# A two-layer encoder on one core: low parts of weights issued later, gate blocks reordered, convolution taps issued sooner

## The chip, the cores and the metric

One NeuronCore of a Trainium2 chip runs the whole program. The metric is the device time of one execution in microseconds (us). Engines are named as in the profile: PE (TensorE's matrix multiplies; PEld its weight loads), DVE (VectorE), ACT (ScalarE), POOL (GpSimd) and SP (SyncE, which issues the DMAs).

## What is computed

Two sequences, of 256 and 512 tokens and 1024 channels, go through the same two layers. A layer, cut to what matters here:

```
h = rms_norm(x);  q, k, v, u, gl = split(h @ w_in)
a = attention(rope(rms_norm(q)), rope(rms_norm(k)), v)         # 8 heads, 2 key heads
z = u[:1024] * sigmoid(u[1024:])                               # the gated input of the convolution
z = depthwise_conv(z, 31 taps) + b;  c = silu(layer_norm(z)) @ w_pw
x = x + (sigmoid(gl_a) * a + sigmoid(gl_c) * c) @ w_out
x = x + ffn(rms_norm(x))
```

All of it is fp32. A product is computed from split operands: each operand is a high part (rounded to the PE's fast format) and a low part (the rest), and three passes (high by high, low by high, high by low) go into one PSUM bank.

## The kernel before

Channels lie on the 128 partitions, in eight blocks of 128 channels; the 768 tokens lie along the free axis. The program is emitted by a planner (class Clock, line 54): it keeps a planned time `now`, moved on by each matmul's columns at 2400 per us, and a planned DVE time `dve`, moved on by each DVE operation (Vector, line 119: elements / 960 plus 0.13 us, of which a tap's addend is the constant TAP_MORE, line 1650). Every engine then runs its own instructions strictly in the order in which the planner put them out.

**Weights.** A weight block of 128 x 1024 is loaded into a stage tile by SP (Stage.load, line 227). Unit.make (line 240) then puts out, one right behind the other, a copy into the high part on ACT and a subtraction that makes the low part; for the blocks of the projections (names lo_L_wu, lo_L_wgl, lo_L_wqkv, lo_L_wpw) the subtraction is DVE's. `staged` counts the stages that are still in use, and load (line 313) issues the next one while there are fewer than four.

**The stream.** The projections are blocks in an order that FILL (line 1616) writes out by hand. "ag:j" makes channel block j of the convolution's gated input z: two weight blocks, each over all 768 tokens ("ag2" does j = 0 and 1). "gl:n" makes an output gate: one weight block; gates 0 to 7 belong to the heads, 8 to 15 to the convolution's output and go to DRAM. "k", "v" and "q:n" are the attention's projections. The first seven entries (BEFORE, line 1634) run before the attention. The others are its filling: the attention is 48 units (8 heads, 6 token tiles each, named h0t0 to h7t5), and behind the scores and again behind the transposes of each unit fill() (line 1386) puts out FILL_US / 2 planned us of the stream.

**A unit of the attention.** scores (line 1305): three matmuls on PE, the negated row maximum on DVE (L_hXtYst), Exp on ACT with a sum, the sum's reciprocal on POOL (line 1332), the scaling on ACT (L_hXtYp). flip (line 1336), one unit later: PE transposes the scaled block (L_hXtYT, line 207), ACT and DVE make its high and low parts. values (line 1355) multiplies by v and the gate.

**The convolution.** Each channel block needs 30 taps on DVE (conv, line 761: SCALAR_TENSOR_TENSOR on L_y, 128 x 783, in place), which go out in turn from at most two blocks' chains, as long as the planned DVE time is less than 1 us ahead of `now` (tick, line 76). There are three z tiles (N_Z, line 1668). An "ag" block first needs one of them:

Of the kernel before, what the change touches and what calls it, by code (L numbers as in the profile page):

```python
# [118 lines left out]
class Vector:  # L119
# [5 lines left out]
    def __getattr__(self, name):  # L125
        f = getattr(self.engine, name)

        def call(out, *args, **kw):
            n = 1
            for d in (args[0].shape if name == "tensor_reduce" else out.shape)[1:]:  # L130
                n *= d
            self.clock.vector(n / 960.0 + (TAP_MORE if n == CONV_N else 0.13))
            return f(out, *args, **kw)  # L133
# [22 lines left out]
def trunk(tc, x_in, x_tok, w_a, w_qkv, w_pw, w_out, w_gu, w_down, vecs, gqk, rope, y_out):  # L156
    nc = tc.nc
    clock = Clock()
    vector = Vector(nc.vector, clock)

    with ExitStack() as ctx:
# [48 lines left out]
        def act(out, in_, func=AF.Copy, **kw):  # L210
            nc.scalar.activation(out, in_, func, **kw)  # L211

        def sub_lo(engine, lo, x, hi):
            engine.tensor_tensor(lo, x, hi.bitcast(F32), op=ALU.subtract)  # L214
# [6 lines left out]
        class Stage:  # L221


            def __init__(self, name, src):
                self.name, self.src, self.tile, self.last = name, src, None, None
# [5 lines left out]
        class Unit:  # L231
# [2 lines left out]

            def __init__(self, name, stages):
                self.name, self.stages, self.out, self.live = name, stages, None, False
                for stage in stages:
                    stage.last = self

            def make(self, engines):  # L240
                hi = wpool.tile([P, 1024], F32R, name="hi_" + self.name, tag="w", bufs=N_W)
                lo = wpool.tile([P, 1024], F32R, name="lo_" + self.name, tag="w", bufs=N_W)
                stage = self.stages[0].tile
                act(hi, stage)
                n = 1024 // len(engines)
                for i, e in enumerate(engines):
                    sl = slice(i * n, (i + 1) * n)
                    sub_lo(e, lo[:, sl], stage[:, sl], hi[:, sl])
                self.out = (hi, lo)

        class Quarter(Unit):

# [6 lines left out]
            def make(self, engines):  # L259
                src = self.quad.operand(self.m)  # L260
                both = wpool.tile([P, 1024], F32R, name="wq_" + self.name, tag="w", bufs=N_W)
                hi, lo = both[:, :512], both[:, 512:]
                act(hi, src)
                sub_lo(engines[0], lo, src, hi)
                self.out = (hi, lo)

        class Quad:

# [19 lines left out]
        class Weights:  # L288
# [36 lines left out]
            def split(self, engines=(nc.gpsimd,)):  # L325
                w = self.all[self.ready]
                while not self.here(w):
                    assert self.load()
                assert self.live + w.size + max(self.staged, N_WS) <= N_W
                self.live += w.size  # L330
                w.live = True
                w.make(engines)
                self.staged -= sum(stage.last is w for stage in w.stages)
                self.ready += 1
                self.next = max(self.next, clock.now + W_STEP[w.size - 1])

            def pump(self):
                while self.load():
                    pass
                if self.ready < len(self.all) and clock.now >= self.next:  # L340
                    w = self.all[self.ready]
                    if self.here(w) and self.live + w.size + max(self.staged, N_WS) <= N_W:
                        self.split(self.engines(w))
# [5 lines left out]
            def get(self, w):  # L349
                while w.out is None:  # L350
                    self.split(self.engines(self.all[self.ready]))
                return w.out

            def free(self, w):
# [60 lines left out]
        weights = Weights()  # L415
# [217 lines left out]
        def layer_blocks(l):  # L633
# [127 lines left out]
            def conv(j, z):  # L761
                wcol = lambda k: vcol(l, V_WDW, k * KC + j)

                def first():
                    y.y[j] = UC(nm(f"y{j}"))
                    act(y.y[j], z[:, :CONV_N], AF.Identity, scale=wcol(0), bias=vcol(l, V_BDW, j))
# [23 lines left out]
                def ready():  # L790
                    first()
                    clock.at(FIRST_AT[1], lambda: clock.waiting.append(taps))
                clock.at(FIRST_AT[0], ready)

# [45 lines left out]
            def gl_body(idx):  # L840
                def body(ws):
# [3 lines left out]
                    for s, (t0, n) in enumerate(SPLITS):  # L845
                        pg = yield from proj_a(ws[0], y.hT, s, nm(f"gl{idx}_{s}"))
                        act(sg[:, t0:t0 + n], pg[:, :n])
                        if s == 0 and FILL[-1] == f"gl:{idx}":
                            y.h_free = 1
# [9 lines left out]

            for b in FILL:  # L860
                kind, _, n = b.partition(":")
# [435 lines left out]
        def attention(y):  # L1297
# [7 lines left out]
            def scores(n):  # L1305
# [22 lines left out]

                late = stream.done((l, FILL[-1]))
                jobs[n] = [  # L1330
# [55 lines left out]
            def fill():  # L1386
                goal[0] += FILL_US / 2
                if not stream.done((l, FILL[-1])):
                    stream.run(goal[0], (l, FILL[-1]))
                    if stream.done((l, FILL[-1])):  # L1390
                        goal[0] = stream.work
                        goal[0] += PW_START
                        y.late = clock.now + 8.0
                        y.h_free = 2
                        split_z(y)
                elif y.m_done:
                    goal[0] = max(goal[0] + (LATE_US - FILL_US) / 2, stream.work)
                    stream.run(goal[0], (l, f"pw:{min(y.m_done, PW_MAX) - 1}"))
# [21 lines left out]
        def channel_norm(y):  # L1420
# [59 lines left out]
            def scale(j):  # L1480
                def f():
                    for s, (t0, n) in enumerate(SPLITS):
                        sl = slice(YO[s], YO[s] + n)
                        vector.tensor_tensor(ys[j][:, sl], ys[j][:, sl], rstd[s][:, :n], op=ALU.mult)
                    if j in SILU_AT:
                        clock.at(0.5, lambda: silus(j))
                return f

            def silus(j1):
                split_z(y)  # L1490
                for j in range(y.silus, j1 + 1):
                    act(ys[j], ys[j], AF.Silu, scale=vcol(l, V_LNG, j), bias=vcol(l, V_LNB, j))
                    y.silus += 1
                    split_z(y)
                if y.silus == KC:
                    y.normed()
# [116 lines left out]
        clock.drain()  # L1613


FILL = ["ag2", "k", "q:0", "gl:0", "ag:4", "ag:2", "ag:3", "gl:8", "v", "gl:9", "gl:1", "q:1", "ag:5", "ag:6",
        "gl:10", "gl:2", "q:2", "ag:7", "gl:3", "gl:14", "gl:12", "gl:4", "gl:11", "q:3", "gl:5", "gl:13", "gl:7",
        "gl:15", "gl:6"]
SILU_AT = (5, 7)
FIRST_AT = (1.2, 1.4)  # L1620
BURSTS = ((1, 7), (6, 4), (5, 2), (3,))
D_FIRST = (4.0, 6.0)
# [11 lines left out]
BEFORE = 7  # L1634
SIG_MAX = 3
SIG_LEFT = 25
FILL_US = 6.3
LATE_US = 3.7
PW_MAX = 10
PW_START = 3.0  # L1640
# [6 lines left out]
RSTD_AFTER = 5.4  # L1647
TABLES_AT = 16.0
TAP_AHEAD = 1.0
TAP_MORE = 0.13  # L1650
W_STEP = (0.9, 2.9)
A_EXP = 2.2
A_REC = (3.5, 2.5)
# [91 lines left out]
```

If all three are in use (line 797), the taps of the oldest chains are put out at once, until one chain is finished; behind them POOL gets the three MEMSETs that clear the new tile's margins (line 803), which wait for the last tap of the chain that had the tile. When all eight chains have been added up (L_ysum), channel_norm (line 1420) puts out mean, squares, variance and scale with steps on PE, DVE, ACT and POOL. The first product with w_pw (pw_body, line 892) needs all of it: clock.force (line 99) puts out what is left.

## Time and profile before

| | us |
|---|---|
| median of 3 runs (2438.95 to 2444.44) | 2441.3 |
| the profiled execution | 2443.3 |
| its span on the core | 2441.5 |
| PE busy in the span | 2226.4 (91%) |
| DVE busy in the span | 1876.5 (77%) |

A row of a timeline gives the start and the length in us, the engine, the line, the operation, what it writes and reads, how many are merged into the row (x16), and in brackets how long the engine had been idle before it and what ended that. A row of the waits gives the engine that waited, for what, the us in total, how often, and the longest. "L_" stands for either layer.

### The profile page before, as it was taken

What the parts mean: (1) busy time and instruction counts of PE and PEld (TensorE: products, weight loads), DVE (VectorE), ACT (ScalarE), POOL (GpSimd) and SP (SyncE); (2) the same over time, 40 slices, a digit from 0 to 9 for tenths busy, and PEclk for the clock granted to TensorE, in tenths of its full rate; (3) what the DMA queues carried; (4) which work ended last, traced back from release to release, by engine and by line L of the source; (5) the groups of instructions that cost most, each with busy time, mean ns of one, the idle gap of its engine ahead of it and who ended that gap; (6) DMA issues with size and microseconds to landing.
All of it is one profiled execution on the core that took longest, in us unless ns stands there. A gap on an engine that the chain in (4) does not pass through costs nothing. (4 is left out here: it accounts for less than half of the span.)

```text
span 2441.5 us, 34896 instructions
## 1 busy us (share of the span) xinstructions
PE 2226.4 (91%) x13276; PEld 2095.6 (86%) x13276; DVE 1876.5 (77%) x2484; ACT 1143.8 (47%) x2289; POOL 1068.2 (44%) x935
## 2 busy tenths in 40 slices
PE   8999869949979999999989998698699799999997
PEld 7989859848979999999988898596589799999997
DVE  5899768956387788798968897689553877987888
ACT  5446536555244444444443555465642444444443
POOL 3704132311256666666445142131112666666663
PEclk9999989969989999999999999899799899999998
DMA  4112111213312343343421111112142133333332
GB/s 165 61 57 69 66 39 63 77 43 113 133 49 90 121 144 116 124 145 113 152 85 61 63 63 57 50 63 72 54 146 101 35 121 127 124 130 137 122 123 87
DMA packets 72423, 229.59 MB, mean 94 GB/s; under 512 B 8128, under 2 KB 15296, under 8 KB 72256
## 3 DMA queue, kind: packets, MB, share of 16 engines
q1 hardware_dynamic: 72256, 227.37, 27.1%
q8 instruction: 104, 1.70, 0.3%
q14 instruction: 63, 0.52, 0.1%
HBM read 208.46 MB, written 18.87 MB: 93 GB/s over the span
## 5 line engine op out<-in xcount | busy, mean ns | idle before, releaser
L133 DVE SCALAR_TENSOR_TENSOR L_y<-L_z,vec,L_y 128x783 f32<-128x783 f32 x480 | 496.1, 1077 | 0.8
L214 POOL TENSOR_TENSOR wq_L_wgu_0m<-T_L_wgu,wq_L_wgu_0m 128x512 fp32r<-128x512 f32 x168 | 228.6, 1376 | 173.8 <-ACT wq_L_wgu_0m L211 173.8
L211 ACT ACTIVATE wq_L_wgu_0m<-T_L_wgu 128x512 fp32r<-128x512 f32 x168 | 102.7, 630 | 259.3 <-DVE T_L_wgu L133 208.7
L214 POOL TENSOR_TENSOR wq_L_wgu_0m<-st_L_wgu,wq_L_wgu_0m 128x512 fp32r<-128x512 f32 x126 | 179.3, 1425 | 43.4 <-ACT wq_L_wgu_0m L211 42.7
L203 PE MATMUL L_gl<-L_h1h,hi_L_wgl 128*128 128x512 f32 (+1 forms) x512 | 176.6, 345 | 0.0
L203 PE MATMUL L_gl<-L_h1h,lo_L_wgl 128*128 128x512 f32 (+1 forms) x512 | 173.2, 338 | 0.0
L203 PE MATMUL L_gl<-L_h1l,hi_L_wgl 128*128 128x512 f32 (+1 forms) x512 | 172.9, 338 | 0.0
L203 PEld LDWEIGHTS L_gl<-L_h1h,lo_L_wgl 128*128 128x128 f32 x512 | 97.0, 189 | 11.0
L203 PEld LDWEIGHTS L_gl<-L_h1l,hi_L_wgl 128*128 128x128 f32 x512 | 97.2, 190 | 9.2
L203 PEld LDWEIGHTS L_gl<-L_h1h,hi_L_wgl 128*128 128x128 f32 x512 | 97.0, 190 | 9.1
L203 PE MATMUL L_c<-L_zsl,hi_L_wpw 128*128 128x256 f32 (+1 forms) x256 | 89.2, 348 | 9.5 <-DVE L_zsl L133 9.5
L203 PE MATMUL L_c<-L_zsh,hi_L_wpw 128*128 128x256 f32 (+1 forms) x256 | 92.1, 360 | 4.6 <-ACT L_zsh L211 4.6
L203 PE MATMUL L_ug<-L_h1h,lo_L_wu 128*128 128x256 f32 (+1 forms) x256 | 89.0, 348 | 2.8 <-DVE lo_L_wu L133 2.8
L133 DVE TENSOR_TENSOR L_dl<-L_silu,L_dh 128x384 fp32r<-128x384 f32 x80 | 59.5, 783 | 41.0 <-ACT L_dh L211 41.0
L203 PE MATMUL L_ug<-L_h1h,hi_L_wu 128*128 128x256 f32 (+1 forms) x256 | 90.6, 354 | 0.0
L203 PE MATMUL L_ua<-L_h1h,lo_L_wu 128*128 128x256 f32 (+1 forms) x256 | 88.6, 346 | 1.4 <-DVE lo_L_wu L133 1.4
L203 PE MATMUL L_ua<-L_h1h,hi_L_wu 128*128 128x256 f32 (+1 forms) x256 | 89.7, 350 | 0.0
L203 PE MATMUL L_ug<-L_h1l,hi_L_wu 128*128 128x256 f32 (+1 forms) x256 | 89.5, 349 | 0.0
L211 ACT ACTIVATE wq_L_wgu_0m<-st_L_wgu 128x512 fp32r<-128x512 f32 x126 | 78.5, 623 | 22.8 <-POOL wq_L_wgu_0m L214 19.8
L203 PE MATMUL L_c<-L_zsh,lo_L_wpw 128*128 128x256 f32 (+1 forms) x256 | 88.9, 347 | 0.0
L203 PE MATMUL L_ua<-L_h1l,hi_L_wu 128*128 128x256 f32 (+1 forms) x256 | 88.1, 344 | 0.0
L203 PE MATMUL L_o<-L_mTlo,hi_L_wo 128*128 128x384 f32 x256 | 86.4, 338 | 0.0
(1630 smaller groups left out, 7626.7 us busy)
## 6 DMA issues: line engine op xcount, KB each, us to landing
st_L_wgu<-w_gu SPq DMA_DIRECT2D x88, 512.0 KB, 3.5
st_L_wu<-w_a SPq DMA_DIRECT2D x32, 512.0 KB, 3.5
st_L_wgl<-w_a SPq DMA_DIRECT2D x32, 512.0 KB, 3.5
st_L_wqkv<-w_qkv SPq DMA_DIRECT2D x24, 512.0 KB, 3.5
st_L_wpw<-w_pw SPq DMA_DIRECT2D x16, 512.0 KB, 3.5
st_L_wo<-w_out SPq DMA_DIRECT2D x16, 512.0 KB, 3.6
g_dram<-L_sgl SPq DMA_DIRECT2D x16, 384.0 KB, 3.0
L_gj<-g_dram SPq DMA_DIRECT2D x16, 384.0 KB, 3.8
```

The lines of the kernel that those rows point to most:

```text
L133: return f(out, *args, **kw)
L203: nc.tensor.matmul(out, lhsT, rhs, start=start, stop=stop)
L211: nc.scalar.activation(out, in_, func, **kw)
L214: engine.tensor_tensor(lo, x, hi.bitcast(F32), op=ALU.subtract)
```

## The change

Four things. The low part of a weight unit whose subtraction is DVE's no longer goes out right behind the high part, but LO_AFTER = 1.6 planned us later, or at the latest when the unit is first asked for (get); the stage counts as in use until then. In FILL "gl:8" goes in front of "ag:3" (so it takes its place among the seven blocks before the attention, and "ag:3" becomes the first filling), "ag:6" goes behind "gl:10", and "ag:7" goes behind "gl:3" and "gl:14". FILL_US goes from 6.3 to 6.5. TAP_MORE goes from 0.13 to 0.02, so the planner counts a tap as 0.836 us (783 / 960 + 0.02) where it counted 0.946.

```
+                self.low = lambda: None
...
-                for i, e in enumerate(engines):
-                    sl = slice(i * n, (i + 1) * n)
-                    sub_lo(e, lo[:, sl], stage[:, sl], hi[:, sl])
+
+                def low():
+                    for i, e in enumerate(engines):
+                        sl = slice(i * n, (i + 1) * n)
+                        sub_lo(e, lo[:, sl], stage[:, sl], hi[:, sl])
+                    weights.used(self)
+
                 self.out = (hi, lo)
+                if engines == (vector,):
+                    self.low = clock.later(LO_AFTER, low)
+                else:
+                    low()
...
-                self.staged -= sum(stage.last is w for stage in w.stages)
                 self.ready += 1
                 self.next = max(self.next, clock.now + W_STEP[w.size - 1])
+
+            def used(self, w):
+                self.staged -= sum(stage.last is w for stage in w.stages)
...
                 while w.out is None:
                     self.split(self.engines(self.all[self.ready]))
+                w.low()
                 return w.out
...
-FILL = ["ag2", "k", "q:0", "gl:0", "ag:4", "ag:2", "ag:3", "gl:8", "v", "gl:9", "gl:1", "q:1", "ag:5", "ag:6",
-        "gl:10", "gl:2", "q:2", "ag:7", "gl:3", "gl:14", "gl:12", "gl:4", "gl:11", "q:3", "gl:5", "gl:13", "gl:7",
+FILL = ["ag2", "k", "q:0", "gl:0", "ag:4", "ag:2", "gl:8", "ag:3", "v", "gl:9", "gl:1", "q:1", "ag:5",
+        "gl:10", "ag:6", "gl:2", "q:2", "gl:3", "gl:14", "ag:7", "gl:12", "gl:4", "gl:11", "q:3", "gl:5", "gl:13", "gl:7",
         "gl:15", "gl:6"]
+LO_AFTER = 1.6
...
-FILL_US = 6.3
+FILL_US = 6.5
...
-TAP_MORE = 0.13
+TAP_MORE = 0.02
```

## Rows read from the trace of the kernel before

**Rows 1.** The page, part 1: busy us, share of the span and instructions of each engine
```profile
PE 2226.4 (91%) x13276; PEld 2095.6 (86%) x13276; DVE 1876.5 (77%) x2484; ACT 1143.8 (47%) x2289; POOL 1068.2 (44%) x935
```
**Rows 2.** What PE waited for: us in total over both layers, times, longest
```profile
PE L_h3t0T L207 <- ACT L_h3t0p L211: 42.6, 2, 21.3
PE L_var L203 <- DVE L_sq L133: 40.3, 2, 20.1
...
PE L_h1t5T L207 <- ACT L_h1t5p L211: 13.0, 2, 6.5
...
PE L_h7t4T L207 <- ACT L_h7t4p L211: 2.3, 2, 1.1
```
**Rows 3.** Timeline of POOL, layer 0, around the wait of 21.3 us
```profile
339.29 0.20 POOL L803 MEMSET L_z<- 128x15 f32 x3 [19.29 <-DVE L_y L133]
...
344.59 0.54 POOL L1332 TENSOR_TENSOR L_h3t0st<-L_h3t0st,nones 128x1 f32<-128x1 f32 x1
```
**Rows 4.** Timeline of DVE, the same stretch
```profile
324.03 15.20 DVE L133 SCALAR_TENSOR_TENSOR L_y<-L_z,vec,L_y 128x783 f32<-128x783 f32 x16
...
346.65 1.23 DVE L133 TENSOR_TENSOR lo_L_wgl<-st_L_wgl,hi_L_wgl 128x1024 fp32r<-128x1024 f32 x1 [6.21 <-ACT hi_L_wgl L211]
```
**Rows 5.** Timeline of POOL, layer 0, ahead of the wait of 6.5 us
```profile
256.31 0.20 POOL L803 MEMSET L_z<- 128x15 f32 x3 [12.74 <-DVE L_y L133]
```
**Rows 6.** Busy us by stretch: PE, PEld, DVE, ACT, POOL, PEclk, DMA share, GB/s
```profile
100.00:240.00 140.00, 137.66 (x901) 124.59 (x899) 129.81 (x163) 64.28 (x143) 42.11 (x49) 1.00 0.20 66
240.00:380.00 140.00, 112.18 (x700) 100.47 (x699) 100.70 (x126) 70.69 (x146) 29.23 (x39) 0.90 0.15 51
380.00:484.00 104.00, 104.00 (x679) 94.22 (x678) 94.50 (x117) 59.67 (x130) 33.19 (x32) 1.00 0.22 74
```
**Rows 7.** Timeline of PE, layer 0, from the end of the stream to w_pw
```profile
484.43 1.56 PE L203 MATMUL L_mean<-L_ysum,ones 128*128 128x256 f32 x4 [0.18 <-DVE L_ysum L133]
506.10 2.72 PE L203 MATMUL L_var<-ones,L_sq 128*128 128x2 f32 x12 [20.11 <-DVE L_sq L133]
...
520.56 0.58 PE L203 MATMUL L_c<-L_zsl,hi_L_wpw 128*128 128x256 f32 x1 [4.74 <-DVE L_zsl L133]
```
**Rows 8.** Timeline of PE behind the wait of 21.3 us
```profile
346.64 0.63 PE L203 MATMUL L_ug<-L_h1l,hi_L_wu 128*128 128x512 f32 x1
347.06 0.63 PE L203 MATMUL L_ug<-L_h1h,lo_L_wu 128*128 128x512 f32 x1
...
350.19 0.39 PE L203 MATMUL L_ug<-L_h1l,hi_L_wu 128*128 128x512 f32 x1
350.43 0.39 PE L203 MATMUL L_ug<-L_h1h,lo_L_wu 128*128 128x512 f32 x1
```
**Rows 9.** Timeline of PE, two 256-column matmuls of a gl block
```profile
272.31 0.28 PE L203 MATMUL L_gl<-L_h1h,hi_L_wgl 128*128 128x256 f32 x1
272.43 0.28 PE L203 MATMUL L_gl<-L_h1l,hi_L_wgl 128*128 128x256 f32 x1
```
**Rows 10.** Timeline of DVE: the row maxima of units h4t0 and h4t5
```profile
387.71 0.42 DVE L133 TENSOR_REDUCE L_h4t0st<-L_h4t0s 128x1 f32<-128x256 f32 x1 [0.40 <-PE L_h4t0s L203]
...
433.39 0.68 DVE L133 TENSOR_REDUCE L_h4t5st<-L_h4t5s 128x1 f32<-128x512 f32 x1
```
**Rows 11.** What DVE waited for: low parts behind their high parts
```profile
DVE lo_L_wgl L133 <- ACT hi_L_wgl L211: 44.6, 18, 6.2
...
DVE lo_L_wu L133 <- ACT hi_L_wu L211: 14.9, 12, 2.4
...
DVE lo_L_wqkv L133 <- ACT hi_L_wqkv L211: 11.9, 10, 2.1
```
**Rows 12.** Timeline of PE, layer 0: a low part that is used as it ends
```profile
101.71 0.39 PE L203 MATMUL L_ua<-L_h1h,lo_L_wu 128*128 128x256 f32 x1 [0.57 <-DVE lo_L_wu L133]
```
**Rows 13.** Timeline of POOL, layer 0, where the attention begins
```profile
151.41 0.20 POOL L803 MEMSET L_z<- 128x15 f32 x3 [17.77 <-DVE L_y L133]
162.03 0.55 POOL L1332 TENSOR_TENSOR L_h0t0st<-L_h0t0st,nones 128x1 f32<-128x1 f32 x1 [10.41 <-ACT L_h0t0p L211]
```

More of the change, by code (lines that the diff above doesn't have):

```diff
@@ L265, in make @@
                 self.out = (hi, lo)
+                weights.used(self)
         class Quad:
```

## The prediction

> **What bounds the kernel now.** I read the page's busy shares first: PE works for 2226 of 2441.5 us [rows 1], so only PE's idle time, some 215 us, can be won by moving work about. Then the list of what PE waited for. Its two longest entries lie in both layers, at the same places and of the same length: 21.3 us in front of the transposes of unit h3t0 and 20.1 us in front of the variance; a wait of 6.5 us at h1t5 is third in this phase [rows 2]. The timelines of POOL and DVE say what they are.
>
> The wait at h3t0 is the planner's own. Block "ag:7" needs a z tile while three are in use, so the planner puts out the taps of the oldest chains at once: 16 taps in one run of 15.2 us [rows 4]. POOL meets the MEMSET of the new tile first, waits 19.29 us for the last tap, then does a q block's rotary work, and only at 344.59 the reciprocal of h3t0 that was queued behind it [rows 3]. ACT's scaling and PE's transposes need that reciprocal. What follows is as dear: the planned DVE time is now far ahead, so no taps go out for a while, and DVE idles 6.21 us in front of a low part [rows 4]. The wait at h1t5 has the same cause, "ag:6": the MEMSET waits 12.74 us, DVE's queue is full of taps, the unit's maximum comes late, and with it the reciprocal [rows 5].
>
> The busy time by stretch shows what this does to DVE. In 100 to 240 it is idle for 10.2 of 140 us, in 380 to 484 for 9.5 of 104, but in the stretch with the two waits, 240 to 380, for 39.3 of 140 [rows 6]. That matters because the stream and the convolution end together: PE's last gate block is done at 484.4 and PE waits only 0.18 us for L_ysum. Behind it comes the channel norm's own chain, during which PE has nothing: 20.11 us for the variance and more up to 520.6 [rows 7]. So two chains reach 484 side by side, and both have to come sooner.
>
> **The change part by part.**
>
> *The z tiles asked for later.* How much later is worked out from the code's columns and the trace. Planned lengths at 2400 columns per us: a gl block 8.2, an ag block 16.4, a q or v block 15.4 us. On the chip 512 columns take about 0.24 and 256 about 0.12 us from start to start [rows 8, 9], so a gl block (24 of each) takes 8.6 and PE is some 10% slower than planned. A unit takes (433.39 - 387.71) / 5 = 9.1 us [rows 10], of which 6.3 x 1.1 = 6.9 are filling, so 2.2 are its own. Filling in front of "ag:7": before 5 gl, v and two q, 2 ag = 120 us, or 19.0 units of 6.3; after 6 gl, three qkv, 3 ag = 144 us, or 22.2 units of 6.5. Counted from the program's start, the block has two gl blocks more in front of it ("gl:8" and "ag:3" only change places) and 3.2 units more: 17.2 + 7.0 = 24 us later in PE's work. "ag:6": one gl and 2.2 units, 13.4 us later. "ag:5" comes one unit later, 2 us. The MEMSETs waited 19.29 and 12.74 us [rows 3, 5]. In the 24 us DVE has about 7 us of other work more (two low parts of 1.23 [rows 4], 3.2 units of some 1.4), which leaves 17 us for taps; it also wins back idle time in 240 to 324. So the forced runs are gone, or a few taps long. Bounds for the two waits together, per layer: all 27.8 us go (the half of 42.6 and 13.0 [rows 2]), or half of it stays, if the chains are late all the same. I take all, and put remains under new waits.
>
> *The clock.* Behind the wait of 21.3 us the 512-column matmuls start 0.42 apart until 349.6 and then 0.23 to 0.24 [rows 8]: the granted clock fell to its lower level (1.2 of 2.4 GHz; 0.90 in the mean of this stretch [rows 6]). Some eight matmuls lost 0.2 us each. With the same behind h1t5, about half as long, 3 us per layer go. Bounds 0 and 4.
>
> *DVE has to keep pace.* Its work from 100 to 484 is 129.8 + 100.7 + 94.5 = 325 us [rows 6], and the change adds and removes none. At the idle share of the two undisturbed stretches (19.7 of 244 us, 8%) it needs 353.5 us and ends at 453.5: 30.5 us sooner, just what PE gains (27.8 + 3). So the stretch of the norm behind it stays as it is. Two edits can make DVE faster still. **Low parts later:** DVE waits 44.6 + 14.9 + 11.9 us for high parts of gl, u and qkv blocks over both layers [rows 11], since a low part is queued right behind its high part. With taps in between, part of that goes. **Taps sooner:** one tap takes 15.20 / 16 = 0.95 us [rows 4]. The planner counted 0.946, which on a PE 10% slower than planned leaves DVE short of work; 0.836 fills that. Together at least nothing, at most about 14 us per layer (the undisturbed stretches' share of the waits on high parts). But DVE only has to win where PE then waits less in the norm; I take 4 per layer.
>
> *What gets later.* A low part 1.6 us later is followed by whatever DVE has queued, and PE waits for it only where it is used at once: 0.57 us at 101.71 [rows 12], one of two such places in a layer. At each it can cost 1.6 us and a tap of 0.95, or save the 0.57. The stage's release and so the next load on SP come 1.6 us later too, in front of stores that nothing awaits. "ag:3"'s MEMSET now lies on POOL in front of h0t0's reciprocal; its chain should end at about 151 as now, well before that is due (162) [rows 13]. Its sigmoid falls among the units' exponentials. A fuller DVE queue makes maxima later; the nearest rows are small waits such as h7t4's 1.1 us [rows 2]. Bounds per layer 0 and 10; I take 4. FILL_US keeps the filling at 37 units (242 / 6.5 against 234 / 6.3) although "ag:3" joined it, so the end of the attention keeps its form. The FFN only has its two plain down units touched; nothing.
>
> **Sum.** Per layer -27.8 - 3 - 4 + 4 = -31; twice, -62. Against the profiled execution's 2443.3 us that is 2381; that execution lies 2.0 above the median, so 2379 by the runs. I say 2380.
>
> **The rivals.**
>
> *The wait moves to the norm.* PE comes 31 us sooner, DVE does not, because taps are held back by something else (z gated late, sigmoids flushed late). For it: the two chains end together now [rows 7], so any wait that PE loses and DVE does not comes back there. Against it: 39 of 59 idle us lie in the disturbed stretch [rows 6]. If DVE ends only 12 us sooner, the layers win 12 each: 2417. Chance 0.17.
>
> *The change does not do what it says:* the z tiles come no sooner at the new place, as the chain in front started later too, and half of the 27.8 us reappears at another unit. Then 14 + 2 per layer: 2409. Chance 0.07.
>
> *Slower: the planned norm overtakes the chip.* The planner counts each tap 0.11 us too short; over 240 taps DVE can fall 26 us behind the plan. L_mean and L_var [rows 7] would then stand in PE's queue in front of the last gate blocks, and PE, in order, would wait out the lag and the 20 us there with that filling queued behind. Price: 20 us of filling per layer that now runs before the norm runs after it. It decides if DVE wins back less than 20 of its 59 idle us; with 10 won it is +10 per layer, 2461. Against it: PE is 10% slower than planned, which takes up most of the lag. Chance 0.07. [...]
>
> *Nothing measurable,* gains and new waits equal: 0.04.
>
> **How the numbers follow.** A measurement of this kernel can tell about 0.2%, 4.9 us. The forecast has 0.65, in its own range 2355 to 2403: the lower end if DVE's extra feed shortens the norm's wait by 12 per layer and nothing new appears, the upper if new waits cost 10 per layer and 6 more of the old ones stay. The range that holds 8 in 10 goes on to 2426, past the first two rivals' times, and starts at 2352. Faster: 0.65 + 0.17 + 0.07 = 0.89, of which I keep 0.01 for the slower side, as their prices are unsure; same 0.04; slower 0.07 + 0.01.
>
> **What would show it.** In the profile after, PE's waits at h3t0 and h1t5 are gone or below 3 us; POOL's MEMSET waits in the attention are short; DVE's idle time between the start of the attention and L_ysum falls from 59 to some 30 us; L_mean runs near 453; the wait at L_var is 14 to 20 us. The forecast is wrong if a wait of over 10 us stands in front of another unit, if L_var's wait grows to 35 us, or if L_mean waits for L_ysum with gate blocks left.

## The result, and the profile after

The changed kernel takes 2336.15 us in the median of four runs (2335.30 to 2336.96), where the kernel before took 2442.55 beside it (four runs, 2438.95 to 2444.44). The ratio is 0.9566 with a 95% interval of 0.9549 to 0.9583: faster by 106 us. The forecast had the sign but 62 us only, and the time lies below its range, 2355 to 2403. The profiled execution of after took 2336.18 us, with a span of 2334.4.

The first part of the page, the busy time by engine, answers to [rows 1]:

```profile
PE 2213.9 (95%) x13276; PEld 2087.3 (89%) x13276; DVE 1880.3 (81%) x2484; ACT 1160.7 (50%) x2303; POOL 1085.7 (47%) x935
```

PE does the same 13276 matmuls. Its busy time fell by 12.5 us, beside a granted clock whose mean over the span rose from 0.959 to 0.982 of full speed, and the span by 107.1, so its idle time fell by 94.6. Where, the list of PE's waits says, which answers to [rows 2] (us over both layers, times, longest):

```profile
...
PE L_c L203 <- ACT L_zsh L211: 9.7, 2, 4.8
PE L_c L203 <- DVE L_zsl L133: 9.5, 2, 4.7
...
PE L_h1t3T L207 <- ACT L_h1t3p L211: 6.1, 2, 3.5
...
PE L_h4t5T L207 <- ACT L_h4t5p L211: 4.8, 2, 2.9
...
PE L_h0t0T L207 <- ACT L_h0t0p L211: 3.0, 2, 1.6
```

The waits at h3t0 and h1t5 are gone, as forecast. But the third long one of before, 20.1 us per layer in front of the variance, is gone as well, and of that the forecast took away 4. PE's timeline in layer 0, against [rows 7], shows how:

```profile
432.12 1.45 PE L203 MATMUL L_mean<-L_ysum,ones 128*128 128x256 f32 x4
...
458.44 1.40 PE L203 MATMUL L_var<-ones,L_sq 128*128 128x2 f32 x12
...
466.44 0.82 PE L207 MATMUL L_rstd<-ident,L_rb 128*128 128x128 f32 x6
...
472.10 0.58 PE L203 MATMUL L_c<-L_zsh,hi_L_wpw 128*128 128x256 f32 x1 [4.85 <-ACT L_zsh L211]
```

L_mean stood at 484.43 and now stands at 432.12, 52 us sooner. No bracket stands behind L_mean, L_var and L_rstd: PE had other work in front of each, because the stream's last gate block ends only at 466.2. The norm's chain is no faster (26.3 us from L_mean to L_var, 21.7 before; 40.0 from L_mean to the first product with w_pw, 30.8 before), but it runs beside that work, where before it ran behind it with nothing else to do. DVE's last step of the convolution, in its timeline:

```profile
427.44 0.97 DVE L133 TENSOR_TENSOR L_ysum<-L_ysum,L_y 128x783 f32<-128x783 f32 x1
```

The busy time by stretch, against [rows 6] (columns as there):

```profile
100.00:240.00 140.00, 132.68 (x873) 120.39 (x872) 132.20 (x164) 64.04 (x141) 42.25 (x48) 1.00 0.19 62
240.00:380.00 140.00, 139.80 (x883) 125.54 (x882) 132.79 (x164) 89.95 (x176) 41.39 (x42) 0.99 0.20 67
380.00:426.00 46.00, 43.12 (x300) 39.97 (x299) 44.12 (x55) 29.01 (x71) 25.42 (x25) 0.96 0.20 72
```

DVE idles 7.8 + 7.2 + 1.9 = 16.9 us from 100 to 426; before it was 59 up to 484. The convolution's end came 56 us sooner: some 42 us by less idle time, and 14 because less of DVE's other work lies ahead of it by then, most of it the attention's (36 row maxima had run before, 31 now) and weights' low parts.

### The profile page after: what moved, and what is told of

Its sections match the earlier page's. It is cut to its first block, busy times and chain, and to the rows that moved or that the text cites. A ratio compares the mean times of both kernels' runs of the same rounds, so it can differ in the third digit from the quotient of the medians.

```text
span 2334.4 us, 34909 instructions
## 1 busy us (share of the span) xinstructions
PE 2213.9 (95%) x13276; PEld 2087.3 (89%) x13276; DVE 1880.3 (81%) x2484; ACT 1160.7 (50%) x2303; POOL 1085.7 (47%) x935
## 3 DMA queue, kind: packets, MB, share of 16 engines
q1 hardware_dynamic: 72256, 227.37, 28.6%
## 5 line engine op out<-in xcount | busy, mean ns | idle before, releaser
L133 DVE SCALAR_TENSOR_TENSOR L_y<-L_z,vec,L_y 128x783 f32<-128x783 f32 x480 | 502.0, 1084 | 1.7
L203 PE MATMUL L_o<-L_mThi,hi_L_wo 128*128 128x384 f32 x256 | 86.8, 339 | 0.3 <-ACT L_mThi L211 0.2
```

The lines of the kernel that those rows point to most:

```text
L203: nc.tensor.matmul(out, lhsT, rhs, start=start, stop=stop)
```

## The experiments

Two theories went into them. **"Two waits"** is the forecast's: the later z tiles remove the two waits, the taps and the low parts are worth some 4 us per layer. **"Early end"** was formed on the profile after: the convolution now ends well ahead of the stream, so the norm's chain hides, and it is the taps and the low parts that bring that end forward.

### The three parts, alone and in pairs

The order (here the new FILL together with FILL_US 6.5), the short taps (TAP_MORE 0.02) and the later low parts were put into the kernel before one at a time, and taken out of the changed one, one at a time. The edits, in this order:

```
e1_order_only  before, with the new FILL and      -FILL_US = 6.3    +FILL_US = 6.5
e2_taps_only   before, with                       -TAP_MORE = 0.13  +TAP_MORE = 0.02
e3_low_only    before, with the low-part edit:    +self.low = clock.later(LO_AFTER, low) ...
e4_no_taps     after, with                        -TAP_MORE = 0.02  +TAP_MORE = 0.13
e5_no_low      after, with           -if engines == (vector,):      +if False:
e6_no_order    after, with the old FILL and       -FILL_US = 6.5    +FILL_US = 6.3
```

> The kernel before with the new order of the filling and FILL_US 6.5, old taps, old low parts. Theory 'two waits' (the forecast's: the order takes 27.8 + 3 us per layer, taps and low parts are worth 4 or less): 2375 to 2385 us, the waits at h3t0 and h1t5 below 3 us, and a wait for the variance of 15 to 20 us per layer as before. Theory 'early end' (the convolution now ends some 40 us ahead of the stream, so that the channel norm runs under filling, and it is the taps and the low parts that bring the end forward): 2365 to 2385 us, and again 10 to 20 us of wait for the variance. If the order alone brings the end forward: 2335 to 2350 us and no wait for the variance.

> The kernel before with TAP_MORE 0.02 alone. Theory 'two waits': the waits at h3t0 and h1t5 stay within 3 us of their 21.3 and 6.5 us, at most 4 us per layer come from a shorter norm: 2434 to 2444 us. Theory 'early end': the plan puts more taps out ahead of 'ag:7', so fewer are forced there, and the convolution ends sooner: 2395 to 2425 us, the wait for the variance below 12 us per layer.

> The kernel before with the later low parts alone. Theory 'two waits': 2436 to 2444 us, the waits at h3t0, h1t5 and for the variance as before. Theory 'early end' as the runs now have it (the short planned taps decide when the convolution ends, low parts keep DVE from standing behind ACT and so shorten the units' chains; with the new order they gave 23 us without the short taps and 29 us with them): 2410 to 2430 us, L_mean 5 to 15 us sooner than 484, and still a wait of 15 to 21 us for the variance.

> The changed kernel with the old TAP_MORE 0.13. Theory 'two waits': at most 4 us per layer are lost, 2336 to 2344 us. Theory 'early end': the planner counts each of the 240 taps 0.11 us longer, 26 us per layer, so the convolution ends up to 26 us later, near the end of the stream, and part of the norm lies bare again: 2350 to 2376 us with 5 to 20 us of wait for the variance per layer.

> The changed kernel with every low part queued right behind its high part again. Theory 'two waits': DVE's waits for high parts come back (18 us more in front of the low parts of gl blocks alone, per layer), which costs at most 4 us per layer: 2336 to 2344 us. Theory 'early end': DVE loses some 20 us per layer of feed, but the convolution has about 40 us of room to the end of the stream, of which the norm's chain needs most: 2340 to 2360 us, with a wait for the variance of 0 to 10 us per layer.

> The changed kernel with the old order of the filling and FILL_US 6.3. Theory 'two waits': the waits at h3t0 and h1t5 come back nearly whole, 2390 to 2400 us or more. Theory 'early end': the short taps alone left 4.1 and 1.5 us at these two units, the low parts take off 23 to 29 us of the 2379 us of the short taps alone: 2348 to 2362 us, no wait for the variance, L_mean at 430 to 440, so the order is worth 12 to 26 us only and not the 54 that the forecast gave it.

Measured:

| in the kernel | us | ratio to before, interval |
|---|---|---|
| the order alone (e1) | 2403.3 | 0.9837 [0.9821, 0.9854] |
| short taps alone (e2) | 2379.4 | 0.9737 [0.9722, 0.9751] |
| later low parts alone (e3) | 2425.1 | 0.9926 [0.9912, 0.9941] |
| order and low parts (e4) | 2380.4 | 0.9745 [0.9730, 0.9759] |
| order and taps (e5) | 2364.7 | 0.9681 [0.9667, 0.9696] |
| taps and low parts (e6) | 2341.5 | 0.9589 [0.9575, 0.9603] |

The order, which the forecast made the heart of the change, is worth 39.8 us alone and only 5.3 on top of the other two, which is about what can be told apart. The short taps are worth 63.7 alone and 44.3 on top; the low parts 17.5 alone and 28.6 on top. "Two waits" missed all six times, by 10 us or more. "Early end" has e3 in its range and was near the others: e4 and e5 came out 4 and 5 us above theirs, e6 and e2 7 and 16 us below, so the taps are worth more than it had said. e1 was 18 us slower than either had it: its wait for the variance stayed as both said, but it has new waits that neither counted.

What each leaves of PE's waits says why. The order alone (e1):

```profile
PE L_var L203 <- DVE L_sq L133: 37.3, 2, 18.7
...
PE L_h1t3T L207 <- ACT L_h1t3p L211: 12.5, 2, 6.3
PE L_h6t4T L207 <- ACT L_h6t4p L211: 9.5, 2, 4.7
...
PE L_mean L203 <- DVE L_ysum L133: 6.7, 2, 3.3
```

The waits at h3t0 and h1t5 are gone, but the one for the variance is not, and three new ones take 14.3 us per layer. The new order didn't make the z tiles wholly free in time. POOL's MEMSETs for "ag:6" and "ag:7" in e1, against 12.74 us [rows 5] and 19.29 us [rows 3]:

```profile
269.71 0.20 POOL L803 MEMSET L_z<- 128x15 f32 x3 [9.68 <-DVE L_y L133]
...
344.87 0.20 POOL L803 MEMSET L_z<- 128x15 f32 x3 [12.39 <-DVE L_y L133]
```

But the runs of taps in front of them shrank. DVE's rows just ahead of the two MEMSETs, first "ag:6" in the kernel before (its 16 taps for "ag:7" are in [rows 4]):

```profile
247.66 8.59 DVE L133 SCALAR_TENSOR_TENSOR L_y<-L_z,vec,L_y 128x783 f32<-128x783 f32 x9
```

and then both in e1:

```profile
266.73 2.92 DVE L133 SCALAR_TENSOR_TENSOR L_y<-L_z,vec,L_y 128x783 f32<-128x783 f32 x3
...
340.00 4.81 DVE L133 SCALAR_TENSOR_TENSOR L_y<-L_z,vec,L_y 128x783 f32<-128x783 f32 x5
```

So 9 and 16 taps in one run became 3 and 5. The new wait at h1t3 is of the old kind at another block: POOL waits for the MEMSET of "ag:5", does a q block's rotary work behind it, and reaches the unit's reciprocal 5 us later (e1, POOL):

```profile
233.86 0.20 POOL L803 MEMSET L_z<- 128x15 f32 x3 [4.45 <-DVE L_y L133]
...
238.96 0.54 POOL L1332 TENSOR_TENSOR L_h1t3st<-L_h1t3st,nones 128x1 f32<-128x1 f32 x1
```

The short taps alone (e2), in the old order, first the MEMSET of "ag:7", then PE's waits at the places of before:

```profile
327.62 0.20 POOL L803 MEMSET L_z<- 128x15 f32 x3
```

```profile
PE L_h3t0T L207 <- ACT L_h3t0p L211: 8.2, 2, 4.1
...
PE L_h1t5T L207 <- ACT L_h1t5p L211: 2.8, 2, 1.5
```

This MEMSET has no wait left (the one of "ag:6" still has 7.06 us). With taps handed out sooner the tile is free when the old place of "ag:7" asks for it, and L_var is not in the list; a new wait of 5.3 us per layer stands at h0t0. Either edit takes most of the wait at h3t0; with both, one of them has little left to do, which is why the order adds 5 us only.

Taking the taps out again (e4) brings back the wait for the variance and makes the one at h1t3 longer:

```profile
PE L_var L203 <- DVE L_sq L133: 37.3, 2, 18.6
...
PE L_h1t3T L207 <- ACT L_h1t3p L211: 12.4, 2, 6.2
```

The low parts act in another place. In e5, without them, the wait for the variance stays away, but the units wait longer:

```profile
PE L_h1t3T L207 <- ACT L_h1t3p L211: 9.7, 2, 5.0
...
PE L_h2t4T L207 <- ACT L_h2t4p L211: 8.4, 2, 4.4
...
PE L_h0t0T L207 <- ACT L_h0t0p L211: 6.0, 2, 3.0
```

DVE, whose queue holds the maxima of those units, stands longer behind ACT's high parts there. In layer 0 the maximum of h2t4 starts 7.6 us behind the unit's first matmul in e5 (304.92 against 297.31) and 3.5 us in the changed kernel (292.05 against 288.57). First e5's waits of DVE, then those of the changed kernel, against [rows 11]:

```profile
DVE lo_L_wu L133 <- ACT hi_L_wu L211: 17.7, 8, 4.7
...
DVE lo_L_wgl L133 <- ACT hi_L_wgl L211: 13.0, 11, 2.9
...
DVE lo_L_wqkv L133 <- ACT hi_L_wqkv L211: 6.2, 6, 1.7
```

```profile
DVE lo_L_wu L133 <- ACT hi_L_wu L211: 8.9, 5, 3.1
...
DVE lo_L_wgl L133 <- ACT hi_L_wgl L211: 6.6, 6, 2.1
...
DVE lo_L_wqkv L133 <- ACT hi_L_wqkv L211: 2.3, 3, 0.8
```

### Is it the norm under filling? The norm late, with the convolution early

```
e12_ln_late   after, with   -LN_AFTER = 5.2   +LN_AFTER = 30.0
e9_taps_half  after, with   -TAP_MORE = 0.02  +TAP_MORE = 0.075
```

> The changed kernel with LN_AFTER 30.0: the convolution ends as early as in the changed kernel, but the channel norm is planned 24.8 us later, so L_mean stands at about 458 to 461, a few us ahead of the stream's end. Theory 'early end' (what the short taps give is the norm under filling, not the convolution's end as such): 2365 to 2385 us, with 12 to 20 us of wait for the variance per layer. If the early end is worth something for another reason (a freer VectorE at the end of the attention, fewer forced taps), the wait comes back in part only: 2340 to 2360 us.

> The changed kernel with TAP_MORE 0.075, half way back. If the planner's length of a tap sets the pace of the convolution in proportion, L_mean comes half way between 432 and 462, at 445 to 449. Theory 'early end' (the norm's chain hides under what is left of the stream, about 34 us in the changed kernel; with L_mean at 440 and 442 it still hid, at 462 it did not): 2340 to 2356 us, with 0 to 6 us of wait for the variance per layer. Theory 'two waits', by which the taps' length matters little: within 5 us of 2336, as long as no wait at h3t0 or h1t5 comes back.

e12 took 2376.3 us (0.9731 [0.9713, 0.9749]), 40 us more than the changed kernel and in the range of "early end". Its convolution ends as early (L_ysum done at 427.4, in after 428.4). PE's timeline:

```profile
457.54 1.45 PE L203 MATMUL L_mean<-L_ysum,ones 128*128 128x256 f32 x4
...
478.23 2.72 PE L203 MATMUL L_var<-ones,L_sq 128*128 128x2 f32 x12 [13.97 <-DVE L_sq L133]
483.60 1.51 PE L207 MATMUL L_rstd<-ident,L_rb 128*128 128x128 f32 x6 [2.66 <-DVE L_rb L133]
```

So the early end as such is worth little (e4, where the convolution ends late, took 2380.4); what pays is the norm's start ahead of the stream's end. Of the 40 us, 28 are PE's idle time from L_mean on, the last column of the table below. e9 took 2359.3 us (0.9657 [0.9642, 0.9671]), 3 us above the range of "early end", and shows the same in another way: its L_mean comes at 442.0, sooner than expected, but its stream ends at 457.2, and half of the wait is back:

```profile
PE L_var L203 <- DVE L_sq L133: 21.0, 2, 10.5
```

The kernels in a row, layer 0, worked out from PE's records: the start of L_mean, the end of the last matmul into L_gl (the stream's end), the second less the first (the lead), and PE's idle time (a stretch less what PE's instructions cover) from the first matmul of the gated input to L_mean, and from L_mean to 12 us behind the first product with w_pw:

| kernel | us | L_mean | stream's end | lead | idle ahead | idle behind |
|---|---|---|---|---|---|---|
| before | 2442.6 | 484.4 | 483.8 | -0.6 | 33.2 | 29.7 |
| e3, low parts alone | 2425.1 | 477.8 | 476.4 | -1.3 | 29.2 | 29.0 |
| e1, order alone | 2403.3 | 463.5 | 459.8 | -3.8 | 14.8 | 28.3 |
| e4, no short taps | 2380.4 | 461.8 | 459.5 | -2.3 | 11.5 | 28.3 |
| e2, short taps alone | 2379.4 | 440.4 | 478.7 | 38.3 | 23.1 | 9.8 |
| e12, norm late | 2376.3 | 457.5 | 463.8 | 6.3 | 13.2 | 23.7 |
| e5, no later low parts | 2364.7 | 442.5 | 476.5 | 34.1 | 18.5 | 9.6 |
| e9, taps half | 2359.3 | 442.0 | 457.2 | 15.1 | 10.2 | 20.2 |
| e15, TAP_MORE 0.04 | 2346.2 | 437.1 | 462.0 | 24.9 | 12.4 | 12.7 |
| after | 2336.2 | 432.1 | 466.2 | 34.0 | 13.0 | 9.6 |
| e14, TAP_MORE 0.0 | 2336.8 | 426.6 | 472.7 | 46.1 | 15.1 | 5.5 |
| e10, TAP_MORE -0.05 | 2361.0 | 428.8 | 481.9 | 53.1 | 21.9 | 6.6 |

The first column is the median of the runs, the others are from the profiled execution (for e14 the slowest of its four, 2342.6 us). The last column falls with the lead, from 29.7 to 5.5, whichever edit made the lead; e10 alone, with the longest, has 1.1 more than e14. The one before it falls with the order, the taps or the low parts, and rises again where the taps crowd DVE's queue. e5 and the changed kernel have the same lead and the same idle time behind L_mean, so what the low parts add to the other two is not lead: in the profiled executions PE idles 14 us less ahead of L_mean over both layers, some 7 us less at units h6t3 to h6t5 behind the norm, and is busy for 7 us less.

### How short may the planned tap be?

```
e10_taps_neg  after, with  -TAP_MORE = 0.02  +TAP_MORE = -0.05
e14_taps_00   after, with  -TAP_MORE = 0.02  +TAP_MORE = 0.0
e15_taps_04   after, with  -TAP_MORE = 0.02  +TAP_MORE = 0.04
```

> The changed kernel with TAP_MORE -0.05, so that the planner counts a tap 0.77 us, where VectorE takes 0.95 and PE runs 10% behind its plan. Theory 'early end': VectorE was idle for 23.5 us only between the first tap and L_ysum, so little can be won, and it cannot keep the plan: its queue runs full, maxima and low parts come later, 2338 to 2370 us, with waits at the units of 15 us or more per layer in all and L_mean waiting for L_ysum by 3 to 15 us with gate blocks behind it. The forecast's slower rival in its pure form (the planned norm overtakes the chip): 2360 us or more, with most of it in front of L_mean and the variance.

> The changed kernel with TAP_MORE 0.0, a tap counted 0.82 us. Theory 'pace': with PE 10% behind its plan this is 0.90 us of the chip's time where a tap takes 0.95, so VectorE falls behind by at most 12 us over 240 taps, and it had only 23.5 us of idle time left: the convolution ends 0 to 4 us sooner, waits at the units grow: 2334 to 2346 us. If VectorE's feed is still what bounds the phase: 2325 to 2333 us.

> The changed kernel with TAP_MORE 0.04, a tap counted 0.86 us. Theory 'pace': 0.94 us of the chip's time, what a tap takes, so VectorE neither falls behind nor waits: 2330 to 2342 us, L_mean within 4 us of 432, still no wait for the variance. If the way from 0.02 (2336) to 0.075 (2359) is even: 2342 to 2348 us with some of that wait back.

e10: 2361.0 us (0.9664 [0.9649, 0.9678]), in the range of both its theories. e14: 2336.8 (0.9569 [0.9555, 0.9583]). e15: 2346.2 (0.9606 [0.9592, 0.9621]). The way from 0.02 to 0.075 is roughly even, with no flat part at 0.04, so "pace" missed e15 by 4 us. The best lies at 0.0 to 0.02, which can't be told apart, and past it the loss is not where the forecast's slower rival had put it. In e10, PE waits 0.2 us for L_ysum in front of L_mean and not at all for the variance, with 53 us of stream left; what it waits for is units, whose maxima stand in DVE's queue behind taps (the maximum of h2t4 starts 9.3 us behind the unit's first matmul, where the changed kernel has 3.5):

```profile
PE L_h2t4T L207 <- ACT L_h2t4p L211: 11.6, 2, 5.9
PE L_h1t3T L207 <- ACT L_h1t3p L211: 11.2, 2, 6.3
```

### Rate or depth of the queue

Short planned taps let more of them out; so does a queue that may run further ahead (TAP_AHEAD).

```
e13_ahead  after, with  +TAP_MORE = 0.13   +TAP_AHEAD = 5.0
e16_deep   after, with  +TAP_MORE = 0.075  +TAP_AHEAD = 5.0  +LN_AFTER = 2.5
e17_mid    after, with  +TAP_MORE = 0.05   +TAP_AHEAD = 3.0
```

> The changed kernel with the old length of a tap (TAP_MORE 0.13) and TAP_AHEAD 5.0 instead of 1.0, so that the planner hands taps out 5 us ahead of its clock. Theory 'pace': what holds the convolution back is the rate at which the planner spends VectorE's time, and a deeper queue shifts each tap by 4 us at most: L_mean at 457 to 462, a wait for the variance of 16 to 19 us, 2370 to 2390 us. Theory 'depth': VectorE runs dry for lack of queued taps, and some five more of them in the queue fill its idle time: L_mean at 430 to 445, 2340 to 2360 us.

> The changed kernel with TAP_MORE 0.075, TAP_AHEAD 5.0 and LN_AFTER 2.5: a longer planned tap, but a deeper queue, and the mean sooner behind L_ysum. With the old length the deeper queue brought L_ysum from 462 to 444 and the idle time ahead of L_mean down to 7 us. If depth and planned length do the same thing in two ways (they hand VectorE taps sooner), L_mean comes at 426 to 436, PE idles 8 to 10 us ahead of it and 9 to 13 us from there to the start of the output projection, 2325 to 2340 us. If the deeper queue only makes up for the planned length and its maxima wait behind taps as at TAP_MORE 0.0: 2337 to 2355 us.

> The changed kernel with TAP_MORE 0.05 and TAP_AHEAD 3.0. If depth and planned length can stand for each other, this lies where the changed kernel lies, L_mean at 428 to 436, no wait for the variance, 2330 to 2342 us. If only the planned length counts near its best value: 2346 to 2354 us, as between 0.04 (2346) and 0.075 (2359), with 2 to 8 us of wait for the variance.

e13: 2358.0 us (0.9649 [0.9633, 0.9665]), in the range of "depth", with L_mean between the two theories: L_ysum is done at 443.9, where e4, the same with a queue of 1 us, had 461.8. The planner's rate isn't all, then; a part of DVE's idle time was a queue run dry. Its L_mean stands 7 us behind L_ysum, at 450.8, with 8.1 us of lead, and 12.3 us of wait for the variance:

```profile
471.60 2.72 PE L203 MATMUL L_var<-ones,L_sq 128*128 128x2 f32 x12 [12.31 <-DVE L_sq L133]
```

e16 and e17 took 2343.0 (0.9582 [0.9567, 0.9596]) and 2342.9 us (0.9583 [0.9567, 0.9599]), with L_mean at 433.0 and 432.4: depth and length can stand for each other, within a few us. Neither is faster than the changed kernel: e17 is 1 us above the range for that, e16 3 us, as its idle time ahead of L_mean did not become shorter (12.8 us in layer 0).

### Smaller edits

```
e7_fill_us    after, with  -FILL_US = 6.5   +FILL_US = 6.3
e8_gl8_back   after, with  "ag:3" in front of "gl:8" again
e11_norm_gap  after, with  -LN_AFTER = 5.2  +LN_AFTER = 2.5   -RSTD_AFTER = 5.4  +RSTD_AFTER = 4.0
```

> The changed kernel with FILL_US 6.3 instead of 6.5. Theory 'two waits': the units come 3% sooner against the filling, the z tiles are asked for one unit later, nothing waits for them any more: within 5 us of 2336, and more filling is left for the norm. Theory 'early end': the same, and with 0.2 us less filling per unit the maxima are due sooner, so the waits of 3 us at h1t3 and h4t5 grow by up to 3 us each: 2336 to 2350 us.

> The changed kernel with 'ag:3' in front of 'gl:8' again, so that its z tile is asked for one gl block (8.6 us) sooner. Both theories: little hangs on it, since the first chains' taps have only begun there: 2334 to 2345 us. If the place of 'ag:3' matters, a wait of 2 to 8 us appears at a unit near h0t0 in both layers: 2340 to 2352 us.

> The changed kernel with LN_AFTER 2.5 and RSTD_AFTER 4.0 instead of 5.2 and 5.4. L_ysum is done 3.7 us ahead of L_mean and the reciprocal root 2.6 us ahead of its spreading, and PE waits 9.6 us per layer at the start of the output projection, behind the norm. If the norm's chain sets that wait: 2327 to 2333 us, the two waits at L_c 5 to 8 us per layer. If the sigmoids, exponentials and high parts on ACT set it: 2334 to 2338 us.

e7: 2342.8 us (0.9590 [0.9576, 0.9604]), e8: 2343.2 (0.9594 [0.9575, 0.9613]), e11: 2339.5 (0.9578 [0.9562, 0.9594]). All intervals overlap that of the changed kernel, so none of the three is shown to differ; e7 has a wait of its own, which would be enough for its 7 us:

```profile
PE L_h3t1T L207 <- ACT L_h3t1p L211: 11.5, 2, 5.8
```

In e11 the two waits at L_c fell from 9.6 to 8.8 us per layer and the time did not (2339.5 lies above both its ranges), so the norm's planned pauses are not what is left there. No version was found that beats the changed kernel.

## Why the prediction was right and wrong

**Right: the two waits and what they were.** They vanished, and PE's idle time ahead of L_mean fell from 33.2 to 13.0 us in layer 0. The forecast's 27.8 less 4 of new waits is 23.8, measured 20.2: inside its bounds.

**Half right: what removed them.** The order alone does it about as foreseen (e1): neither wait is in its list, the runs of taps are 3 and 5 long ("gone, or a few taps long"), and PE's idle time ahead of L_mean falls by 18.4 us in layer 0. Its new waits, 14.3 us per layer, are above the forecast's bound of 10. But the order wasn't needed: in the old order short taps leave 4.1 and 1.5 us at the two units (e2), and with the later low parts beside them 4.2 us at h3t0 and nothing at h1t5, with 19.5 us less idle time ahead of L_mean in layer 0 (e6). The forecast gave the taps no part in these waits.

**The step that failed: "DVE only has to win where PE then waits less in the norm; I take 4 per layer", with bounds of 0 and about 14.** Measured, PE's idle time from L_mean to the output projection fell by 29.7 - 9.6 = 20.1 us per layer; e4 gives it back when the taps alone are undone, e12 most of it when the norm alone is put late. Two assumptions made it too small:

- "At the idle share of the two undisturbed stretches (8%)" took that share for a floor. It was the planner's pace: a tap counted 0.946 us on a PE some 10% behind its plan [rows 8, 9]. The forecast says just that one paragraph on ("0.836 fills that"), but did not work it through: 8% of 354 us is 28 us, and DVE now idles 5%, 16.9 us of 326.
- "30.5 us sooner, just what PE gains ... So the stretch of the norm behind it stays as it is" let the two chains move together. Every us by which the convolution comes sooner than the stream is lead, and lead is worth up to 20 us in the norm, since the norm's chain runs whether or not PE has filling beside it. It moved 52 us sooner, the stream 18.

**Left out: h6t0.** The 4.9 us per layer at this unit, behind the norm, went as well (9.9 us over both layers before, no entry now). With the old order and no lead 10.1 of them stay (e3), with the new order and a lead of up to 25 us 2.5 to 2.7 (e1, e4, e9, e12, e15), with the old order and a lead of 36 us none (e6): the order takes most of them, and a long lead does it too.

**The clock: mis-sized.** 3 us per layer were taken, with bounds of 0 and 4; PE's busy time fell by 12.5, 6.2 per layer. That is not the clock alone: in e14's profiled execution the granted clock is 0.981, against 0.982 in the changed kernel, and PE is busy for 2223.5 us, 9.6 more; what else the busy time holds is open. The profile gives the clock as a share of full speed. Behind the wait at h3t0 it was 0.50 from 346.60 to 349.60, and 512 columns started 0.42 to 0.43 us apart, 1200 columns per us, half of what the planner counts. The norm ran at a granted 0.50 too, which the sum didn't count, as it left that wait in place: L_var's twelve small matmuls took 2.72 us behind the 20.11 us of wait [rows 7], and take 1.40 now, with no idle time of PE ahead of them. The granted clock, the third figure from the end, was 0.50 there before and is 1.00 now; the rows of both stretches, before and after:

```profile
506.10:508.80 2.70, 2.70 (x12) 2.63 (x12) 0.00 (x0) 0.00 (x0) 0.00 (x0) 0.50 0.00 0
```

```profile
458.40:459.90 1.50, 1.50 (x15) 1.50 (x14) 0.69 (x2) 1.49 (x2) 0.00 (x0) 1.00 0.00 0
```

**The sum.** For two layers the forecast had 62. By layer 0's numbers the norm adds 2 x 16.1, h6t0 2 x 4.9, the busy time 2 x 3.2, and the idle time ahead of L_mean takes off 2 x 3.6: 103, against 106. Most of the rest is a wait between the layers (PE L_n1var <- DVE L_n1ss), 7.6 us before and 4.9 after: it is 7.5 or 7.6 in every run without the later low parts and 4.9 or 5.0 in every run with them.

**A length in the working.** By the code a gl block is 24 x 512 and 24 x 256 columns, 7.68 planned us and not 8.2, and an ag block 15.4, not 16.4; PE is then 12.5% slower than planned in it. "ag:7" comes 3.0 units later instead of 3.2, and 23 to 24 us instead of 24, so nothing in the forecast hangs on it.

**The rivals.** *The wait moves to the norm:* the other way round. *It does not do what it says:* in part true of the order, which shortened the MEMSETs' waits without ending them and brought a wait of the same kind at h1t3, but at the price of the order alone (e1, 2403). *Slower:* not seen in the changed kernel, and in e10, where the planner counts a tap 0.77 us, the price came in front of the units, some 9 us more ahead of L_mean in layer 0, and not at L_mean and L_var. PE falling behind its plan as DVE does would account for that; it is argued, not shown. The longest wait for L_ysum in front of L_mean in any run is 3.3 us (e1).

Of what the forecast wanted to see, the two waits and the MEMSETs came as said; DVE's idle time (17, not 30), L_mean (432, not 453) and the wait for the variance (0, not 14 to 20) each pointed past it the same way.

Not settled: why the low parts are worth more with the short taps (28.6 us) than alone (17.5). The shorter waits on DVE and the sooner maxima are in the rows; that these make the difference is argued, not shown. The edit also holds each stage tile longer, and no run separates the two.

## What to carry to other kernels

Where a chain of small steps stands between two stages, ask how far ahead of the last independent work it starts: here a us of lead was worth more than half a us on average, up to 35 us of it, although the chain itself took longer. Where a planner writes the order, an engine's idle share can be the planner's doing: one with 8% idle in a quiet stretch may be held back by a planned duration. And when two parts of a change can each remove the same wait, price each alone and each on top of the other, since the sum of the two counts the wait twice.

## What was not expected of the hardware

A tap isn't one length. With none of POOL's rotary products beside them, four take 3.86 us; with those of the k block beside them three take 3.60, and the longest of the three 1.50. Rows of the timeline of the changed kernel, the first stretch with one of POOL's products in it, the second without:

```profile
57.53 3.60 DVE L133 SCALAR_TENSOR_TENSOR L_y<-L_z,vec,L_y 128x783 f32<-128x783 f32 x3
...
58.95 1.35 POOL L711 TENSOR_TENSOR L_kr<-L_kr,L_kt 128x256 f32<-128x256 f32 x1
...
202.10 3.86 DVE L133 SCALAR_TENSOR_TENSOR L_y<-L_z,vec,L_y 128x783 f32<-128x783 f32 x4
```

Of the 480 taps, 77 are longer than 1.2 us in the changed kernel and 64 in the one before. Each of these overlaps one of POOL's rotary products, and no tap without a POOL instruction beside it is longer than 1.04 us (244 and 278 of them). Still, 61 of the 395 taps of at most 1.1 us in the changed kernel overlap a rotary product too, and no run here took the products away, so it is not shown that they are the cause. The mean of all taps is 1.08 us in both kernels, so they have no part in the difference between them.
